# Down projection of a Strassen-like FFN: result tiles taken at the first write, and the combinations of w_out on VectorE, one step ahead of their split

## The chip, the cores and the metric

The kernel runs on one core of one Trainium2 chip. The metric is device time in microseconds of one execution, the median of several runs. One profiled execution gives the trace. The engines are TensorE (PE in the profile), VectorE (DVE), ScalarE (ACT), GpSimd (POOL) and SyncE (SP), which issues the DMAs. Each engine works through its own instructions strictly in order, and engines wait for one another on semaphores.

## The reference

A trunk of two layers on 1024 positions of width 1024, all in fp32. Layer 0 mixes tokens by a gated MLP, layer 1 by RWKV-7; each then has cross-attention to a small memory and a SwiGLU FFN with D_FF = 2816, each part between two RMS norms and added to x. The part that matters here is the FFN, which runs twice:

```python
def swiglu_ffn(x, w_in, w_out):
    gate, up = jnp.split(x @ w_in, 2, axis=-1)
    return (jax.nn.silu(gate) * up) @ w_out
```

The change touches the last product, h @ w_out, with h of 1024 x 2816 and w_out of 2816 x 1024: the down projection.

## The kernel before

**Splits.** Matrix products work on fp32 numbers taken apart into a high and a low part of a shorter format. `split` makes them: ScalarE copies the source into the high part (`wh`, L118), VectorE subtracts it from the source and so gets the low part (`wl`, L119). Three matmuls (high by high, high by low, low by high) then stand for one.

**Seven products.** The down projection divides h and w_out into 2 x 2 blocks and forms seven products of sums of blocks, in Strassen's manner, where plain blocks would need eight. The combinations of h are made in `ffn`, by GpSimd, and written to seven scratch arrays in DRAM (L485 to L501). `ffn_out` does the rest. It runs the products in the order 1, 2, 5, 6, 3, 7, 4. Each has six steps along the inner dimension: the first of one 128-row piece (tiles of 128x512), the five others of two (128x1024). So there are 42 steps, numbered q, and each has 12 or 24 matmuls into four PSUM banks of 128x512, one for each j of 0 to 3. Banks `A` serve products 1, 6, 7 and 4, banks `B` the products 2, 5 and 3.

**One round of the loop, step q:**

- `load(q + 3)` has SyncE fetch the step's piece of h into a `wr` tile (three buffers, L596). In products 1, 2, 5 and 6 it also fetches a piece of w_out into an `a32` tile (L600), kept for the products after. Each of these four products brings in one of the four blocks of w_out.
- `unit(q + 1)` first makes the combination of w_out that the step needs, in place, as the difference of two kept pieces: L609 in product 5, L611 in 6, L613 in 7, L615 in 4. The engine `E` is GpSimd. It then splits the piece of h (`wl<-wr`) and that of w_out (`wl<-a`); there are buffers for two steps' parts.
- `mm` (L634) does the matmuls of step q, and after a product's last step `evac` takes the four banks' results into the result tiles `y`: a copy by ScalarE in products 1, 5 and 6, an addition by VectorE in products 2 (L657), 3 (L664) and 7 (L667).
- A result half that is final goes to `finish`: ScalarE sums its squares (L646), VectorE multiplies it by a gain (L647), and when a tile is whole, a closing task for the norm and the addition to x is queued and worked off in `tick`.

**Buffers.** All 128x1024 fp32 tiles of this part (`a32`: h's tiles, pieces of w_out, results) come from one pool, `A`, of 32 buffers. Whoever takes one waits until its last user is done. The eight result tiles are taken at the start of `ffn_out` (L588).

**Order.** The program's text gives the order in which work is handed out, but a scheduler in the compiler's front end orders each engine's instructions by a simulated timeline. A change in one place can so reorder instructions elsewhere.

In the second FFN (`by_tile`) the last product runs tile by tile at the end, with splits that stay resident.

## Time and profile before

| | us |
|---|---|
| median of 3 runs (3232.7 to 3247.02) | 3232.87 |
| the profiled execution's own time | 3235.78 |
| its span, first to last instruction | 3234.0 |
| first down projection, on TensorE | about 1081 to 1320 |
| second down projection, on TensorE | about 2992 to 3226 |
| mean granted clock of TensorE | 0.969 |

The page of the profile gives for each engine its busy time, share of the span and instructions. Groups of instructions read "line, engine, operation, out<-in, shapes, count | busy us, mean ns of one | idle time before them and what ended it". Timeline rows read "start, duration, engine, line, operation, count [idle time before <- what ended it]". Rows of waits read "who waits <- for whom: us in total, times, longest". Rows of windows give the busy time of engines in a stretch, TensorE's granted clock, the DMA share and the rate.

### The profile page before, as it was taken

Reading aid. Unit: us, or ns where it says so; the run is one execution under the profiler, and the core shown is the slowest. Engines: PE = TensorE matmul, PEld = TensorE weight load, DVE = VectorE, ACT = ScalarE, POOL = GpSimd, SP = SyncE. Lnnn points to the kernel's source line nnn. Section 1 sums busy time; section 2 is a strip of 40 time slices with the busy share of each in tenths; the row PEclk is TensorE's granted clock in tenths of the full one; section 3 lists DMA queues with packets and bytes.
Section 4 is the critical chain, followed back from the end, with each engine's and each line's share of the span. In section 5 each row is a group of like instructions: output and inputs, shape, how many; then the busy total and the mean of one; then the engine's idle time right before and its main releaser. Section 6 shows DMA issues by size and latency. Waiting matters only on the chain. (4 is left out here: it accounts for less than half of the span.)

```text
span 3234.0 us, 44200 instructions
## 1 busy us (share of the span) xinstructions
PE 3082.2 (95%) x16570; PEld 2514.8 (78%) x16570; DVE 1864.5 (58%) x2626; ACT 1484.1 (46%) x2751; POOL 1033.2 (32%) x810
## 2 busy tenths in 40 slices
PE   8999999899999989999989899999999899999998
PEld 6888888778888767878767788887788688887776
DVE  5563544665555486655765677565545755554766
ACT  5442544533333335666753355465545533332433
POOL 0100011365555270111421443333011655554441
PEclk9999999999999999999998889799999999999999
DMA  5622644423333634644866634535554233333633
GB/s 190 206 74 70 199 125 154 143 73 103 101 98 100 249 123 130 203 140 144 263 197 191 186 95 111 142 96 186 176 164 155 66 102 98 98 104 129 220 103 138
DMA packets 432502, 456.56 MB, mean 141 GB/s; under 512 B 77664, under 2 KB 307200, under 8 KB 432288
## 3 DMA queue, kind: packets, MB, share of 16 engines
q1 hardware_dynamic: 425376, 428.57, 41.9%
q0 software_dynamic: 6912, 25.17, 2.4%
q8 instruction: 131, 2.15, 0.3%
q14 instruction: 83, 0.68, 0.1%
HBM read 331.43 MB, written 122.22 MB: 140 GB/s over the span
## 5 line engine op out<-in xcount | busy, mean ns | idle before, releaser
L119 DVE TENSOR_TENSOR wl<-wr,wh 128x1024 fp32r<-128x1024 f32 (+1 forms) x417 | 514.7, 1244 | 472.9 <-ACT wh L118 472.0
L438 PE MATMUL ps<-a,wh 128*128 128x512 f32 x2464 | 771.0, 398 | 8.4 <-DVE a L119 6.2
L118 ACT CAST wh<-wr 128x1024 fp32r<-128x1024 f32 (+1 forms) x417 | 371.2, 902 | 638.1 <-PE ps L634 194.9
L438 PEld LDWEIGHTS ps<-a,wh 128*128 128x128 f32 x2464 | 464.8, 189 | 125.9 <-DVE a L119 8.0
L438 PE MATMUL ps<-a,wl 128*128 128x512 f32 x1232 | 479.7, 398 | 0.0
L148 PE MATMUL ps<-a,wh 128*128 128x512 f32 (+1 forms) x848 | 328.6, 392 | 13.1 <-ACT a L118 9.6
L148 PE MATMUL ps<-wh,a 128*128 128x512 f32 x800 | 315.8, 402 | 12.4 <-ACT t L1159 3.3
L150 PE MATMUL ps<-a,wl 128*128 128x512 f32 (+1 forms) x848 | 325.0, 385 | 1.6 <-DVE wl L119 1.5
L149 PE MATMUL ps<-a,wh 128*128 128x512 f32 (+1 forms) x848 | 324.9, 384 | 1.1 <-DVE a L119 1.1
L149 PE MATMUL ps<-wl,a 128*128 128x512 f32 x800 | 318.6, 398 | 0.6 <-DVE wl L119 0.6
L150 PE MATMUL ps<-wh,a 128*128 128x512 f32 x800 | 316.4, 399 | 0.0
L208 POOL TENSOR_TENSOR sm<-sm,mhalf 128x4 f32<-128x4 f32 (+3 forms) x60 | 71.7, 1196 | 676.4 <-DVE sm L228 606.3
L438 PEld LDWEIGHTS ps<-a,wl 128*128 128x128 f32 x1232 | 232.8, 189 | 57.4 <-DVE wl L119 0.9
L634 PE MATMUL ps<-wl,wh 128*128 128x512 f32 x588 | 236.0, 401 | 21.2 <-DVE wl L119 21.1
L119 DVE TENSOR_TENSOR wl<-s,wh 128x512 fp32r<-128x512 f32 x176 | 200.2, 1151 | 64.0 <-ACT wh L118 60.4
L634 PE MATMUL ps<-wh,wl 128*128 128x512 f32 x588 | 233.1, 396 | 0.0
L634 PE MATMUL ps<-wh 128*128 128x512 f32 x588 | 197.1, 398 | 18.1 <-ACT wh L118 13.0
L148 PEld LDWEIGHTS ps<-a,wh 128*128 128x128 f32 x848 | 162.2, 192 | 45.8 <-ACT a L118 10.5
L118 ACT CAST wh<-s 128x512 fp32r<-128x512 f32 x176 | 106.3, 619 | 198.9 <-PE ps L438 70.9
L150 PEld LDWEIGHTS ps<-a,wl 128*128 128x128 f32 x848 | 162.4, 192 | 35.9 <-DVE wl L119 2.8
L148 PEld LDWEIGHTS ps<-wh,a 128*128 128x128 f32 x800 | 151.6, 190 | 49.7 <-ACT t L1159 3.8
L149 PEld LDWEIGHTS ps<-a,wh 128*128 128x128 f32 x848 | 163.1, 192 | 31.8 <-DVE a L119 1.5
(281 smaller groups left out, 5562.0 us busy)
## 6 DMA issues: line engine op xcount, KB each, us to landing
scr<-a SPq DMA_DIRECT2D x218, 256.0 KB
wr<-in_ffn_w_in SPq DMA_DIRECT2D x90, 512.0 KB
wr<-scr SPq DMA_DIRECT2D x70, 512.0 KB
scr<-t SPq DMA_DIRECT2D x60, 512.0 KB
wr<-in_rw_w_rkv SPq DMA_DIRECT2D x48, 512.0 KB
a<-in_ffn_w_out SPq DMA_DIRECT2D x40, 512.0 KB
t<-scr SPq DMA_DIRECT2D x36, 512.0 KB
ld<-scr SPq DMA_DIRECT2D x72, 256.0 KB
```

The source lines that it names most:

```text
L118: self.nc.scalar.copy(hi, src)
L119: (engine or self.nc.vector).tensor_sub(lo, src, hi)
L148: nc.tensor.matmul(out, lhsT=ah, rhs=bh, start=start, stop=False)
L149: nc.tensor.matmul(out, lhsT=ah, rhs=bl, start=False, stop=False)
L150: nc.tensor.matmul(out, lhsT=al, rhs=bh, start=False, stop=stop)
L208: self.nc.gpsimd.tensor_tensor(out=r, in0=v, in1=self.mhalf[:, 0:n], op=ALU.pow)
L438: self.nc.tensor.matmul(out, lhsT=a, rhs=b, start=start and k == 0 and (i == 0), stop=k == 3 and i == 2, skip_group_check=True)
L634: nc.tensor.matmul(ps, lhsT=a, rhs=b, start=i in (1, 2, 5) and n == 0 and k == 0 and z == 0, stop=n == NS - 1 and k == steps[n][1] - 1 and ...
```

## The change

Two edits in `ffn_out`, made together.

First, the result tiles: `y` starts empty, and `evac` takes a tile from pool `A` when it is first written, in product 1 (upper row of blocks) and in product 5 (lower row).

Second, the combinations: they leave `unit` for a function of their own, `combine`, which uses VectorE. The loop calls it for step q + 2, ahead of `unit(q + 1)`. So a combination is handed out one round before the split that reads it.

```diff
-        y = [self.a32() for _ in range(NT)]
+        y = {}
...
-        def unit(q, resident=False):
+        def combine(q):
+
             i, n = seq[q]
-            K = steps[n][1]
-            N = K * 512
-            w = lambda b, a: W[b, a, n][:, :N]
-            E = nc.gpsimd
+            w = lambda b, a: W[b, a, n][:, :steps[n][1] * 512]
+            E = nc.vector
             if i == 5:
                 E.tensor_sub(w(0, 0), w(0, 1), w(0, 0))
             elif i == 6:
...
             elif i == 4:
                 E.tensor_sub(w(1, 0), w(1, 0), w(0, 0))
+
+        def unit(q, resident=False):
+            i, n = seq[q]
+            K = steps[n][1]
+            N = K * 512
+            w = lambda b, a: W[b, a, n][:, :N]
             src = {1: (0, 0), 5: (0, 0), 6: (0, 0), 2: (1, 0), 4: (1, 0), 3: (1, 1), 7: (0, 1)}[i]
...
         def evac(i, j, A, B):
             o = lambda r, c: y[2 * j + r][:, c * 512:c * 512 + 512]
+            if i in (1, 5):
+                y[2 * j + i // 5] = self.a32()
             if i == 1:
...
                 load(q + AHEAD)
+            if q + 2 < len(seq):
+                combine(q + 2)
             if q + 1 < len(seq):
                 unit(q + 1, by_tile and seq[q + 1][0] == 4 and seq[q + 1][1] < NS - 2)
```

In the changed kernel the combinations stand at L608, L610, L612 and L614, `mm` at L639, the squares at L651, the gain at L652, the additions at L664 (product 2), L671 (3) and L674 (7). Each pass has 24 combinations; 24 instructions so leave GpSimd and 24 join VectorE.

How the program's order on an engine moves is shown below; a row has the line, the operation, the tiles with their numbers (`out<-in`), and the shape. Tile numbers differ between the two programs.

The first place is VectorE in the first FFN, at the end of product 2 and the start of product 5. Before: the splits of product 5's first step, then the additions and gains of product 2's results with the splits of the second step between them.

```order
L119 TENSOR_TENSOR wl_8582<-wr_8504,wh_8581 128x512
L119 TENSOR_TENSOR wl_8586<-a_8174,wh_8585 128x512
L657 TENSOR_TENSOR a_8162<-ps_8416,a_8162 128x512
L657 TENSOR_TENSOR a_8164<-ps_8420,a_8164 128x512
L647 TENSOR_TENSOR a_8162<-a_8162,gb_8170 128x512
L657 TENSOR_TENSOR a_8166<-ps_8424,a_8166 128x512
L647 TENSOR_TENSOR a_8164<-a_8164,gb_8170 128x512
L657 TENSOR_TENSOR a_8168<-ps_8428,a_8168 128x512
L119 TENSOR_TENSOR wl_8633<-wr_8540,wh_8632 128x1024
L647 TENSOR_TENSOR a_8166<-a_8166,gb_8170 128x512
L119 TENSOR_TENSOR wl_8637<-a_8178,wh_8636 128x1024
```

The same place of the change (L664 are the additions, L652 the gains).

```order
L119 TENSOR_TENSOR wl_8579<-wr_8500,wh_8578 128x512
L119 TENSOR_TENSOR wl_8583<-a_8166,wh_8582 128x512
L610 TENSOR_TENSOR a_8166<-a_8729,a_8166 128x512
L664 TENSOR_TENSOR a_8374<-ps_8412,a_8374 128x512
L614 TENSOR_TENSOR a_8286<-a_8286,a_8166 128x512
L664 TENSOR_TENSOR a_8382<-ps_8416,a_8382 128x512
L652 TENSOR_TENSOR a_8374<-a_8374,gb_8162 128x512
L664 TENSOR_TENSOR a_8390<-ps_8420,a_8390 128x512
L652 TENSOR_TENSOR a_8382<-a_8382,gb_8162 128x512
L664 TENSOR_TENSOR a_8398<-ps_8424,a_8398 128x512
L119 TENSOR_TENSOR wl_8630<-wr_8536,wh_8629 128x1024
L119 TENSOR_TENSOR wl_8634<-a_8170,wh_8633 128x1024
```

The first combinations of products 6 (L610) and 4 (L614) have come in among the additions; the one for product 4 is made here already. Those of product 5 (L608) and the first three of product 7 (L612) stand some rows further up, between product 2's splits.

The second place is VectorE at steps 1 to 3 of product 6. Before: splits alone, that of h's piece and that of w_out's in turn.

```order
L119 TENSOR_TENSOR wl_8851<-wr_8767,wh_8850 128x1024
L119 TENSOR_TENSOR wl_8855<-a_8178,wh_8854 128x1024
L119 TENSOR_TENSOR wl_8876<-wr_8804,wh_8875 128x1024
L119 TENSOR_TENSOR wl_8880<-a_8182,wh_8879 128x1024
L119 TENSOR_TENSOR wl_8913<-wr_8845,wh_8912 128x1024
L119 TENSOR_TENSOR wl_8917<-a_8194,wh_8916 128x1024
```

The same place of the change, from the second of these splits to the fifth.

```order
L119 TENSOR_TENSOR wl_8856<-a_8170,wh_8855 128x1024
L610 TENSOR_TENSOR a_8186<-a_8848,a_8186 128x1024
L612 TENSOR_TENSOR a_8626<-a_8848,a_8626 128x1024
L119 TENSOR_TENSOR wl_8877<-wr_8801,wh_8876 128x1024
L610 TENSOR_TENSOR a_8214<-a_8873,a_8214 128x1024
L612 TENSOR_TENSOR a_8655<-a_8873,a_8655 128x1024
L119 TENSOR_TENSOR wl_8881<-a_8174,wh_8880 128x1024
L614 TENSOR_TENSOR a_8402<-a_8402,a_8186 128x1024
L610 TENSOR_TENSOR a_8250<-a_8910,a_8250 128x1024
L612 TENSOR_TENSOR a_8692<-a_8910,a_8692 128x1024
L614 TENSOR_TENSOR a_8430<-a_8430,a_8214 128x1024
L119 TENSOR_TENSOR wl_8914<-wr_8846,wh_8913 128x1024
```

Two combinations stand ahead of the splits of step 2, two between them, and four ahead of those of step 3, which read `a_8848`, `a_8873` and `a_8910`, the last three pieces of w_out to be loaded.

The third place is SyncE at the start of the first down projection. Before: the store of h's last parts (`scr`) and the loads of w_out.

```order
L369 DMA t4_9331<-scr2_93 128x1024
L490 DMA scr12_4981<-a_8115 128x512
L491 DMA scr14_4983<-a_8115 128x512
L600 DMA a_8174<-in_ffn_w_out 128x512
L495 DMA scr15_4984<-a_8153 128x512
L600 DMA a_8178<-in_ffn_w_out 128x2x512
```

The same place of the change.

```order
L369 DMA t4_9332<-scr2_93 128x1024
L490 DMA scr12_4981<-a_8115 128x512
L491 DMA scr14_4983<-a_8115 128x512
L600 DMA a_8166<-in_ffn_w_out 128x512
L495 DMA scr15_4984<-a_8153 128x512
L600 DMA a_8170<-in_ffn_w_out 128x2x512
```

Only the numbers of the tiles have moved.

## The prediction

> **What bounds the kernel now.** First the page: the share of each engine, and the chain that ended last.

> ```profile
> span 3234.0 us, 44200 instructions
> PE 3082.2 (95%) x16570; PEld 2514.8 (78%) x16570; DVE 1864.5 (58%) x2626; ACT 1484.1 (46%) x2751; POOL 1033.2 (32%) x810
> PE 35%; DVE 3%; DMA 2%; ACT 1%; issue 1%; POOL 0%; SPq 0%; DVEq 0%; POOLq 0%; ACTq 0%
> ```

> TensorE is busy for 95% of the span, so an edit that removes no matmul can win only from the remaining 152 us of idle time and from a low clock. Next, what TensorE waits for in the down projection (L634), over the whole span; the columns are total us, times and the longest wait.

> ```profile
> PE ps L634 <- DVE wl L119: 21.1, 18, 2.7
> PE ps L634 <- ACT wh L118: 13.0, 3, 6.4
> PE ps L634 <- DVE a L657: 5.1, 6, 1.4
> ```

> That is 39 us in two passes, and no row has GpSimd as releaser: where the combinations are made, TensorE waits for a split (`wl`) or for an addition into a result tile (`a`, L657), both on VectorE. The timeline of TensorE shows where these waits lie in the first pass (seven of the ten after 1130 us; in brackets the idle time).

> ```profile
> 1133.65 0.50 PE L634 MATMUL ps<-wl,wh 128*128 128x512 f32 x1 [0.42 <-DVE wl L119]
> 1145.53 0.47 PE L634 MATMUL ps<-wh 128*128 128x512 f32 x1 [1.44 <-DVE a L657]
> ...
> 1152.09 0.49 PE L634 MATMUL ps<-wl,wh 128*128 128x512 f32 x1 [0.98 <-DVE wl L119]
> 1159.37 0.50 PE L634 MATMUL ps<-wl,wh 128*128 128x512 f32 x1 [1.54 <-DVE wl L119]
> 1186.08 0.50 PE L634 MATMUL ps<-wl,wh 128*128 128x512 f32 x1 [1.86 <-DVE wl L119]
> 1199.41 0.50 PE L634 MATMUL ps<-wl,wh 128*128 128x512 f32 x1 [0.52 <-DVE wl L119]
> ...
> 1212.75 0.50 PE L634 MATMUL ps<-wl,wh 128*128 128x512 f32 x1 [0.90 <-DVE wl L119]
> ```

> They form two zones, and the waits by window give their sums: 1130 to 1165 us (end of product 2, product 5), then 1183 to 1215 us (product 6), then the same zones of the second pass (3042 to 3080, where the L657 row repeats, and 3094 to 3127).

> ```profile
> PE ps L634 <- DVE wl L119: 2.9, 3, 1.5
> PE ps L634 <- DVE a L657: 2.5, 3, 1.4
> PE ps L634 <- DVE wl L119: 4.2, 4, 1.9
> PE ps L634 <- DVE wl L119: 3.3, 3, 1.5
> PE ps L634 <- DVE wl L119: 4.4, 4, 2.0
> ```

> Why VectorE is late there: groups of its splits in 1110 to 1215 us, where the combinations run, and in 1215 to 1244 us, where none does; then one place in the timeline.

> ```profile
> L119 DVE TENSOR_TENSOR wl<-a,wh 128x1024 fp32r<-128x1024 f32 x15 | 38.8, 2589 | 0.4 <-ACT wh L118 0.4
> L119 DVE TENSOR_TENSOR wl<-a,wh 128x1024 fp32r<-128x1024 f32 x5 | 6.1, 1220 | 0.2 <-ACT wh L118 0.2
> 1181.49 3.46 POOL L611 TENSOR_TENSOR a<-a 128x1024 f32<-128x1024 f32 x1 [15.43 <-DMA a<-in_ffn_w_out]
> 1182.89 3.14 DVE L119 TENSOR_TENSOR wl<-a,wh 128x1024 fp32r<-128x1024 f32 x1 [0.20 <-ACT wh L118]
> 1185.95 3.38 DVE L119 TENSOR_TENSOR wl<-wr,wh 128x1024 fp32r<-128x1024 f32 x1
> ```

> The same split takes 1.22 us alone and 3.4 us beside a GpSimd combination. While both engines run, VectorE falls behind; that is the bound of these zones, about 20 us of idle time in all.

> **The change part by part.** *Taking result tiles late* frees eight of 32 buffers while product 1 begins. The 6.4-us waits at the start of each pass are for `wh`, and ACT in its turn had waited for the first w_out load:

> ```profile
> 1080.62 0.62 ACT L118 CAST wh<-a 128x512 fp32r<-128x512 f32 x1 [7.59 <-DMA a<-in_ffn_w_out]
> ```

> In SyncE's order that load still stands behind the same write of h's parts, and the matmuls it waits for are the same. So I take 0. The bounds are 0 and a gain of the whole 13.0 us; a loss is excluded, since no load is placed later.

> *Moving the combinations* takes 48 instructions off GpSimd and puts as many of the same shapes on VectorE. GpSimd's groups of 12 run from 2.84 to 3.10 us each:

> ```profile
> L613 POOL TENSOR_TENSOR a<-a 128x1024 f32<-128x1024 f32 (+1 forms) x12 | 37.1, 3104 | 0.0
> L611 POOL TENSOR_TENSOR a<-a 128x1024 f32<-128x1024 f32 (+1 forms) x12 | 34.1, 2843 | 43.9 <-DVE wl L119 28.4 <-DMA a<-in_ffn_w_out 15.4
> ```

> No combination runs on VectorE before. The nearest rows are its own fp32 subtractions of the same shapes, undisturbed:

> ```profile
> 1175.59 0.69 DVE L119 TENSOR_TENSOR wl<-wr,wh 128x512 fp32r<-128x512 f32 x1 [2.65 <-ACT wh L118]
> 1221.20 1.23 DVE L119 TENSOR_TENSOR wl<-wr,wh 128x1024 fp32r<-128x1024 f32 x1
> 1222.34 1.22 DVE L119 TENSOR_TENSOR wl<-a,wh 128x1024 fp32r<-128x1024 f32 x1
> ```

> Back to back they start 1.14 us apart; the small shape's pair 0.6 us. The ends for one combination are 1.14 us and, if it ran as on GpSimd, 3.4 us; I take 1.14, the row of the same engine and operation. Per pass this adds 20 x 1.14 + 4 x 0.6 = 25 us to VectorE, and takes away 15 x (2.59 - 1.22) = 20 us on the `a` splits and about 14 us on the `wr` splits, which are slowed alike. So VectorE gets no busier; what matters is where the combinations stand.

> *Zone of product 5.* Idle is 5.4 us in the first pass and 5.8 in the second. Each wait also restarts TensorE slowly: its first matmul takes 0.50 us instead of 0.39 and the next start slips, 0.28 us a wait, six waits, 1.7 us. Together 7.1 and 7.5 us. After: the last result of product 2 ends about 1143.7 on TensorE; VectorE adds it (0.6), then makes the two splits of step 1 (2 x 1.14), ending 1146.7. TensorE would ask for them at 1146.0, so one wait of about 0.8 us stays, 1.1 with its restart. The five others go: their splits now precede the demand by 1 to 2 us. Saved **6.0 and 6.4 us**.

> *Zone of product 6.* Idle 4.2 and 4.4, four restarts 1.1, and the clock fell after the longest wait. Windows of 2 us, with TensorE's busy time, granted clock, DMA share and GB/s, first at a wait of 1.54 us, then after that of 1.86:

> ```profile
> 1158.00:1160.00 2.00, 0.63 (x3) 1.00 0.53 206
> 1186.00:1188.00 2.00, 1.92 (x6) 0.72 0.47 167
> 1188.00:1190.00 2.00, 2.00 (x6) 0.50 0.33 127
> 1190.00:1192.00 2.00, 2.00 (x10) 0.92 0.67 242
> 1186.88 0.61 PE L634 MATMUL ps<-wl,wh 128*128 128x512 f32 x1
> ...
> 1190.28 0.41 PE L634 MATMUL ps<-wh,wl 128*128 128x512 f32 x1
> ```

> In the last two rows eight starts lie 0.425 us apart instead of 0.227: 1.6 us lost. The zone costs 6.9 and 7.1 us. The waits of 1.44 and 1.54 us left it at 1.00, so I take 1.54 as safe.

> [...]

> After: nine combinations stand among the first splits of product 6. From 1182.89: the split of step 1 ends 1184.05, when TensorE asks (1184.2): no wait. Two combinations, a split, two combinations, the split of step 2: six at 1.14 end 1190.9; TensorE asks at 1189.5, a wait of 1.4. Four combinations and two splits end 1197.8; it asks at 1196.6, 1.2. Later splits have nothing ahead of them. 2.8 us with restarts stay, no wait as long as 1.54, so the clock holds. Saved **4.1 and 4.3 us**.

> *Waits added.* A combination of product 5 or of 7 waits on VectorE for its w_out load, and the splits queue behind it, then TensorE. Two places:

> ```profile
> 1117.96 17.89 POOL L609 TENSOR_TENSOR a<-a 128x512 f32<-128x512 f32 x6 [36.78 <-DMA a<-in_ffn_w_out]
> 1176.71 1.49 SPq L600 DMA_DIRECT2D a<-in_ffn_w_out  x3
> ```

> Before, the operands were there at 1117.96 and then kept pace with six combinations; VectorE reaches its first at 1119 and the sixth about 1129. The three last loads were in use from 1181.49, and VectorE reaches them at 1184.05. So 0, with 2.5 us of slack; beyond it each us late is a us lost.

> *The rest.* The wait of up to 2.7 us at product 3, and what else stays of the `wl` row, stands beside the closing work, not touched: 0. The scheduler also reorders parts of the RWKV layer; there the largest wait (1400 to 2500 us) is

> ```profile
> PE ps L148 <- ACT a L118: 10.2, 4, 5.4
> ```

> and the waits add to some 50 us. I take 0, with 5 us either way, a tenth of them.

> Sum: 6.0 + 6.4 + 4.1 + 4.3 = 20.8 us. The profiled execution took 3235.8 us (span 3234.0 and 1.8 around it): 3215.0. It lies 2.9 above the median of 3232.87, so the forecast is **3212**, -0.6%. A difference below 0.5% (16 us) can hardly be told from none.

> **The rivals.** *Half is given back.* The two waits left in product 6 last longer than 1.5 us and the clock falls once or twice in each pass (1.6 us each, 3 to 6 in all), or the saving of the first pass shrinks at the DMA-bound places of the next layer, and only 10 to 14 us come: 3219 to 3222, within 0.5%. For it: the margins above are 0.1 to 1.4 us. Against it: the second pass has nothing behind it.

> *Slower: a combination is as dear on VectorE as on GpSimd.* Then the burst of product 6 decides. TensorE's waits at steps 2 and 3 are each four combinations and two splits less one step of TensorE (24 matmuls, 5.45 us): 4c + 2.28 - 5.45 for a combination of c us. At 1.14 that is the 1.4 above, at 3.4 it is 10.4 twice, 21 us a pass with 0.6 for restarts and 1.6 or more for the clock, against 7 before, and the 20 us more of VectorE use up the gain at product 5 too. Two passes: 3233 + 2 x 17 = 3267. The gain of the two passes, 20.8, is gone when 16 x (c - 1.14) reaches it: at 2.4 us. Against it: the undisturbed rows at 1.22.

> *VectorE stops at a load.* If the last three loads land later than 1184.05 on that clock, the combinations wait, with them the splits of steps 1 to 3, and TensorE loses each us one to one. The gain of a pass is gone when they land at 1194; at 1200 in both passes the time is 3212 + 2 x 16 = 3244. For it: on SyncE they stand behind loads of h that wait for splits. Against it: in the profile they are issued 4.8 us before first use, and their order stays.

> *The late result tiles do pay:* the first loads gain their buffers earlier and the 6.4-us waits go: 3212 - 13 = 3199. Against it: SyncE's order.

> **How the numbers follow.** Forecast as summed, within 5 us: 0.56. Half given back: 0.24. Dear combinations: 0.04. Stopped at a load: 0.08. Result tiles pay: 0.08. The range 3201 to 3229 takes in the forecast, half given back and the small cases of either; it leaves out the dear combinations, most of the stop, and the lower end of the last. Faster by over 0.5% (below 3216.7) holds the forecast but for its upper edge, and the last rival: 0.61; within 0.5%: half given back, that edge and the milder stops, 0.31; slower: 0.08.

> **What would show it.** Right: no GpSimd work from these lines; splits at 1.22 us in both zones; combinations at 1.2 us; waits of L634 on `wl` at about 10 us instead of 21, on the additions near 0, on `wh` still 13; granted clock 1.00 in product 6. Wrong: combinations over 2 us, a DMA of w_out as a releaser on VectorE, waits for `wh` gone, or new waits of TensorE in the RWKV layer.

## The result and the profile after

| | before | after |
|---|---|---|
| median of 9 runs, us | 3240.79 | 3220.90 |
| all runs, us | 3232.7 to 3250.6 | 3208.5 to 3226.1 |
| profiled execution, us (span) | 3235.78 (3234.0) | 3209.03 (3207.3) |
| first pass, first to last matmul of `mm`, us | 233.05 | 221.76 |
| second pass, us | 234.08 | 220.83 |
| from the first pass to the second, us | 1678.2 | 1675.2 |

The ratio of the runs is **0.993, 95% interval 0.9912 to 0.9948**: faster by 0.7%, where 3212 of 3232.87, 0.9935, was forecast. Both medians lie 8 to 9 us above the values that the prediction started from and arrived at, 3232.87 and 3212, since its three runs of the kernel before lay low. A few runs of these kernels took over 5900 us; they are left out of every median and ratio here.

The page of the kernel after, its span and engines:

```profile
span 3207.3 us, 44170 instructions
PE 3071.3 (96%) x16570; PEld 2511.4 (78%) x16570; DVE 1829.9 (57%) x2674; ACT 1484.9 (46%) x2751; POOL 893.0 (28%) x762
```

GpSimd has lost its 48 instructions and 140 us; VectorE has 48 more and is busy 35 us less. The waits of TensorE in the down projection (L639 now) over the whole span:

```profile
PE ps L639 <- ACT wh L118: 13.2, 3, 6.4
...
PE ps L639 <- DVE wl L119: 11.9, 9, 2.7
```

The waits for `wh` stay at 13; those for `wl` fall from 21.1 to 11.9, and the row of the additions into result tiles after product 2 (5.1 before) is gone. The timeline of TensorE has these waits of 0.3 us and more in the first pass, after the 6.43 at its start:

```profile
1184.59 0.50 PE L639 MATMUL ps<-wl,wh 128*128 128x512 f32 x1 [1.09 <-DVE wl L119]
1191.40 0.50 PE L639 MATMUL ps<-wl,wh 128*128 128x512 f32 x1 [1.05 <-DVE wl L119]
1243.59 0.50 PE L639 MATMUL ps<-wl,wh 128*128 128x512 f32 x1 [2.63 <-DVE wl L119]
1258.01 0.50 PE L639 MATMUL ps<-wl,wh 128*128 128x512 f32 x1 [1.49 <-DVE wl L119]
```

Nothing is left in the zone of product 5, two waits in that of product 6, and the long one of product 3 is as before. VectorE's groups show why: splits in 1110 to 1205 us, then two of the four groups of combinations over the whole span.

```profile
L119 DVE TENSOR_TENSOR wl<-wr,wh 128x1024 fp32r<-128x1024 f32 x15 | 18.3, 1220 | 17.3 <-ACT wh L118 17.2
L119 DVE TENSOR_TENSOR wl<-a,wh 128x1024 fp32r<-128x1024 f32 x15 | 18.3, 1218 | 0.4 <-ACT wh L118 0.4
L612 DVE TENSOR_TENSOR a<-a 128x1024 f32<-128x1024 f32 (+1 forms) x12 | 13.4, 1128 | 0.0
L608 DVE TENSOR_TENSOR a<-a 128x1024 f32<-128x1024 f32 (+1 forms) x12 | 13.1, 1129 | 0.0
```

In the kernel before, 15 splits of each kind took 2.59 (`wl<-a`) and 2.18 us (`wl<-wr`) in 1110 to 1215 us. VectorE did not stand idle ahead of these combinations (0.0), and by 0.1 us in all ahead of the other two groups: none waited for its load.

### The profile page after: what moved, and what is told of

Same layout as the page of the kernel before. It is cut to its first block, busy times and chain, and to the rows that moved or that the text cites. A ratio compares the mean times of both kernels' runs of the same rounds, so it can differ in the third digit from the quotient of the medians.

```text
span 3207.3 us, 44170 instructions
## 1 busy us (share of the span) xinstructions
PE 3071.3 (96%) x16570; PEld 2511.4 (78%) x16570; DVE 1829.9 (57%) x2674; ACT 1484.9 (46%) x2751; POOL 893.0 (28%) x762
## 5 line engine op out<-in xcount | busy, mean ns | idle before, releaser
L119 DVE TENSOR_TENSOR wl<-wr,wh 128x1024 fp32r<-128x1024 f32 (+1 forms) x417 | 477.6, 1155 | 480.1 <-ACT wh L118 477.3
L118 ACT CAST wh<-wr 128x1024 fp32r<-128x1024 f32 (+1 forms) x417 | 371.1, 901 | 621.3 <-PE ps L639 172.3
L148 PE MATMUL ps<-a,wh 128*128 128x512 f32 (+1 forms) x848 | 328.3, 392 | 11.2 <-ACT a L118 7.9
L148 PE MATMUL ps<-wh,a 128*128 128x512 f32 x800 | 314.5, 401 | 11.7 <-ACT t L1168 3.0
L438 PEld LDWEIGHTS ps<-a,wl 128*128 128x128 f32 x1232 | 233.0, 189 | 57.2 <-DVE wl L119 0.9
L639 PE MATMUL ps<-wl,wh 128*128 128x512 f32 x588 | 231.9, 394 | 11.9 <-DVE wl L119 11.9
L119 DVE TENSOR_TENSOR wl<-s,wh 128x512 fp32r<-128x512 f32 x176 | 199.8, 1149 | 67.5 <-ACT wh L118 64.2
L639 PE MATMUL ps<-wh,wl 128*128 128x512 f32 x588 | 229.9, 391 | 0.0
L639 PE MATMUL ps<-wh 128*128 128x512 f32 x588 | 194.8, 394 | 13.2 <-ACT wh L118 13.2
L118 ACT CAST wh<-s 128x512 fp32r<-128x512 f32 x176 | 106.4, 620 | 199.7 <-PE ps L438 66.7
L148 PEld LDWEIGHTS ps<-a,wh 128*128 128x128 f32 x848 | 162.1, 192 | 44.3 <-ACT a L118 8.8
L148 PEld LDWEIGHTS ps<-wh,a 128*128 128x128 f32 x800 | 151.3, 189 | 48.5 <-ACT t L1168 3.5
```

Source lines behind the costliest of these rows:

```text
L118: self.nc.scalar.copy(hi, src)
L119: (engine or self.nc.vector).tensor_sub(lo, src, hi)
L148: nc.tensor.matmul(out, lhsT=ah, rhs=bh, start=start, stop=False)
L438: self.nc.tensor.matmul(out, lhsT=a, rhs=b, start=start and k == 0 and (i == 0), stop=k == 3 and i == 2, skip_group_check=True)
L639: nc.tensor.matmul(ps, lhsT=a, rhs=b, start=i in (1, 2, 5) and n == 0 and k == 0 and z == 0, stop=n == NS - 1 and k == steps[n][1] - 1 and ...
```

## The experiments

**The result tiles alone.** The kernel before with `y = {}` and the tile taken in `evac`:

```diff
-        y = [self.a32() for _ in range(NT)]
+        y = {}
...
+            if i in (1, 5):
+                y[2 * j + i // 5] = self.a32()
```

> The kernel before with the late result tiles alone. Theory of the prediction: worth nothing, within 2 us of the kernel before; the two waits of L634-like matmuls for wh at the start of the passes stay at 6.4 us each, and the ten waits on VectorE after 1130 us stay at 19.9 us in all. Rival (the tiles give the first loads their buffers): the waits for wh go, 13 us faster.

Measured: 1.0005 of before (0.9991 to 1.0019). TensorE's waits in its profile, over the whole span:

```profile
PE ps L634 <- DVE wl L119: 21.7, 17, 4.0
PE ps L634 <- ACT wh L118: 12.8, 2, 6.4
...
PE ps L634 <- DVE a L659: 5.1, 6, 1.5
```

They are those of before. This edit is worth nothing by itself, and the rival falls. One wait differs, 4.0 us where before had 1.86, and its place shows what the order of the two engines' starts did. The timeline of GpSimd, VectorE and TensorE at step 1 of product 6:

```profile
1182.82 2.41 POOL L611 TENSOR_TENSOR a<-a 128x1024 f32<-128x1024 f32 x1 [15.28 <-DMA a<-in_ffn_w_out]
1182.95 3.37 DVE L119 TENSOR_TENSOR wl<-wr,wh 128x1024 fp32r<-128x1024 f32 x1 [4.57 <-ACT wh L118]
1189.65 0.80 PE L634 MATMUL ps<-wl,wh 128*128 128x512 f32 x1 [3.95 <-DVE wl L119]
```

Here GpSimd began 0.13 us ahead of the step's first split, and that split took 3.37 us. In the kernel before it had begun 0.03 us behind it (1181.49), and the split ran undisturbed:

```profile
1181.46 1.22 DVE L119 TENSOR_TENSOR wl<-wr,wh 128x1024 fp32r<-128x1024 f32 x1 [4.58 <-ACT wh L118]
```

So TensorE waited 2.1 us longer here. In both cases the one that began second took longer, by about what the other still had to do: here the split, 3.37 us instead of 1.22, with 2.28 us of the GpSimd instruction to come; in the kernel before GpSimd, 3.46 us instead of 2.41, with 1.19 us of the split to come. What the two engines share is not shown by these runs.

**VectorE, but no step ahead.** The kernel before with one word changed:

```diff
-            E = nc.gpsimd
+            E = nc.vector
```

> The kernel before with the combinations on VectorE, but still handed out in the round of their split, and the result tiles taken up front. Theory (the engine is what counts, since splits beside a GpSimd combination take 3.4 us instead of 1.2): as the change, 20 to 25 us faster than before in the profile, about 0.993; waits on the first additions gone, two waits of about 1 us at product 6 in each pass. Rival (the step ahead is what counts): a combination directly ahead of its split delays it by 1.14 us or more at each of 24 steps, so that half of the gain or more is missing, 3222 or slower.

Measured: 0.9954 (0.9933 to 0.9975). The passes take 222.4 and 222.6 us, 22 less than before together. Of the waits in 1130 to 1215 us one row is left:

```profile
PE ps L634 <- DVE wl L119: 2.1, 2, 1.1
```

This is the row of the change. The scheduler hoists the combinations on VectorE by itself, to nearly the same places: the first ones of the burst in product 6 start at 1179.93, in the change at 1177.64, both right behind a split of w_out's piece. The median, 3223.8, is some 3 us above that of the change, and the intervals overlap: the step ahead adds nothing that these runs can tell.

**One step ahead, but on GpSimd.** The change with its engine set back, and the tiles up front:

```diff
-            E = nc.vector
+            E = nc.gpsimd
...
-        y = {}
+        y = [self.a32() for _ in range(NT)]
```

> The kernel before with the combinations one step ahead, still on GpSimd. Theory: the splits still run beside GpSimd combinations at 3.4 us, so nothing is won: within 5 us of before, waits of the down projection on VectorE 17 to 23 us as before. Rival (TensorE waits because a combination comes late): most of the gain of the change, 15 us or more.

Measured: 1.0015 (0.9994 to 1.0035); passes of 234.0 and 234.2 us; waits for splits of 20.3 us over the span. First the splits in 1110 to 1215 us, then the waits in 1130 to 1218:

```profile
L119 DVE TENSOR_TENSOR wl<-a,wh 128x1024 fp32r<-128x1024 f32 x15 | 38.8, 2588 | 0.4 <-ACT wh L118 0.4
PE ps L639 <- DVE wl L119: 7.2, 7, 1.9
PE ps L639 <- DVE a L662: 2.6, 3, 1.5
```

Splits and waits are those of before. The rival falls: that the combination came late was not the trouble.

**No combinations at all.** The four branches are taken out of the kernel before:

```diff
-            if i == 5:
-                E.tensor_sub(w(0, 0), w(0, 1), w(0, 0))
...
-                E.tensor_sub(w(1, 0), w(1, 0), w(0, 0))
```

> The kernel before with all 48 combinations of w_out left out (the products use the uncombined blocks). Theory: every wait of the two zones goes, with restarts and clock 14 us in each pass, 28 us: about 3208 in the profile, some 4 us less than the change; splits at 1.22 us throughout. Rival (VectorE is slow there for another reason, such as the w_out loads arriving at 390 GB/s): splits of 1110 to 1140 us still above 2 us and waits of 5 us or more left in the zones.

This leaves 48 subtractions out of the computation. Measured: 0.9915 (0.9893 to 0.9936); passes of 219.9 and 220.9 us, and one wait of 0.2 us between 1130 and 1215 us. In 1110 to 1205 us its splits took 1.22 us, with the loads of w_out as before, so it is not the loads that slow them. The combinations thus cost the kernel before 26.3 us in its two passes, and the change wins back 24.5. Part of both is the clock after the wait at product 3, which fell in both passes of before, in one here and in none of the change (last section): at 1.7 us each, 24.6 and 21.1 us remain.

**The change with duplicates on GpSimd.** Each combination is made a second time, into a tile that nobody reads:

```diff
+        dup = self.s7.tile([P, D], F32, name='s7', tag='s7')
...
+            pair = {5: ((0, 1), (0, 0)), 6: ((1, 1), (0, 0)), 7: ((1, 1), (0, 1)), 4: ((1, 0), (0, 0))}.get(i)
+            if pair:
+                nc.gpsimd.tensor_sub(dup[:, :steps[n][1] * 512], w(*pair[0]), w(*pair[1]))
```

> The change, and GpSimd makes each of the 24 differences of a pass a second time into a spare tile that nobody reads; nothing but buffers of operands waits for it. Theory (VectorE and GpSimd slow each other down whenever both run such subtractions): splits and combinations of VectorE beside the duplicates at 2.5 to 3.4 us again, in 79 us of a pass some 45 instructions of VectorE fewer, less its idle time: TensorE's waits grow by 20 to 45 us a pass, 3250 to 3300. Rival (before, TensorE waited because GpSimd's result came late): nobody waits for the duplicates, within 5 us of the change.

Measured: 1.0147 (1.0118 to 1.0175), median 3287.7. Groups of GpSimd and VectorE, then TensorE's waits, over the span:

```profile
L618 POOL TENSOR_TENSOR s<-a 128x1024 f32<-128x1024 f32 (+1 forms) x48 | 154.0, 3207 | 167.5 <-DVE a L609 87.3 <-DVE a L611 70.7 <-issue 7.0
L615 DVE TENSOR_TENSOR a<-a 128x1024 f32<-128x1024 f32 x10 | 20.8, 2082 | 0.0
L609 DVE TENSOR_TENSOR a<-a 128x1024 f32<-128x1024 f32 x10 | 20.5, 2081 | 0.0
PE ps L643 <- DVE wl L119: 50.5, 17, 6.7
```

Work whose result nobody reads makes the kernel 66 us slower than the change (3221 to 3222 in its two measurements), and no wait of VectorE in the passes names a duplicate as what ended it. VectorE's combinations of products 5 and 4 go from 1.22 to 2.08 us (those of 6 and 7 stay at 1.21), and the waits on its splits from 11.9 to 50.5. Up to half of the 66 us is the clock that fell at the longer waits: summed from the granted clock, 36 us are lost to it in the two passes, 4 in the change.

**Loads six steps ahead.** The w_out part of `load` becomes a function of its own:

```diff
+        def load_w(q):
...
+            if q + 6 < len(seq):
+                load_w(q + 6)
```

> The change with the pieces of w_out loaded six steps ahead instead of three, so that the last three stand on SyncE ahead of the loads of h and the nine combinations of product 6 need not be made in one burst. Theory (the two waits left at product 6 come from the burst): they go, 2.7 us a pass, and nothing else moves: 5 us faster than the change. Rival (VectorE stops at a load): the loads of 1110 to 1130 us already run at 390 GB/s, 1.5 MB more take 4 us, and combinations that stand ahead of product 2's splits wait for them: new waits of TensorE of 1 to 4 us between 1130 and 1145 us, no gain or slower.

Measured: 0.9966 (0.9942 to 0.9989), a median of 3238.1 and so **slower** than the change by 16 us instead of faster by 5, though the intervals overlap. Yet its passes take 219.3 and 219.8 us, and in 3030 to 3150 us one wait is left (none in 1120 to 1235):

```profile
PE ps L643 <- DVE wl L119: 0.3, 1, 0.3
```

So the two waits of product 6 did come from the burst, and no load stops VectorE; the time went elsewhere, into the 1698 us between the passes.

**The first loads early.** In the FFN's last block, ahead of its last stores:

```diff
+            if m == NF - 1:
+                self.W0 = []
...
+                for c, K in ((0, 1), (1, 2), (3, 2))[:3]:
+                    t = self.a32()
+                    nc.sync.dma_start(t[:, :K * 512].rearrange('p (k c) -> p k c', k=K), wv[0][:, c:c + K, 0:512])
+                    self.W0.append(t)
```

> The change with the first three loads of w_out handed out during the last block of the FFN's first half, ahead of the stores of h's last parts on SyncE. Theory (the 6.4-us wait at the start of a pass is for a load that stands too far back in SyncE's order, not for buffers): the wait falls below 2 us, and the low clock after it goes for the most part: 5 to 8 us a pass, 10 to 16 us faster than the change. Rival (the first piece of h or the next pieces of w_out are as late): waits at the first two steps that add to 4 us or more, gain below 5 us in all.

Measured: 0.993 (0.9905 to 0.9956), runs from 3201 to 3238; the median, 3217.2, is 5 us under the change's, where 10 to 16 were expected. The row of waits for `wh` is gone altogether, and the first pass ends at 1295.0 us instead of 1303.9. In the profiled execution, one of 3235.2 us, all of it is lost again between the passes. First the longest wait in 1990 to 2100 us, in the RWKV layer, with its row in the timeline; then TensorE in 5 us ahead of it and in 100 us around it (busy, granted clock, DMA share, GB/s); then the same stretch of the change:

```profile
PE ck L1426 <- DMA x<-scr: 6.2, 1, 6.2
2019.52 0.98 PE L1426 MATMUL ck<-x 32*32 32x32 f32 x50 [6.25 <-DMA x<-scr]
2000.00:2005.00 5.00, 4.53 (x29) 0.58 0.39 120
1995.00:2095.00 100.00, 91.89 (x739) 0.57 0.49 128
2000.00:2100.00 100.00, 95.43 (x1119) 0.95 0.53 140
```

The clock stayed at half for 85 of the 100 us. The wait of 6.2 us did not start this: a mean of 0.58 over 2000 to 2005 puts the fall at about 2000.8, and the wait began at 2013.3.

**The change again.**

> The change once more, as it stands, for the comparison with the two above and for a second profile. Theory: the same waits to 0.2 us (1.1 twice at product 6, 2.6 at product 3), about 0.993 of before. What may differ is the clock: if a stretch of low clock begins only where more than some 1.7 us of one cell of a fixed 3.41-us raster are idle, the 2.6-us wait lowers it in some passes and not in others, and every stretch ends on the same raster. Rival (the length of the wait alone decides): as in the first profile, no low clock after 2.6 us.

Measured: 0.9934 (0.9912 to 0.9956), passes of 221.8 and 221.85 us, the same waits in both zones. In neither pass did the clock fall after the 2.6 us at product 3, so this run by itself does not decide between the two readings of the clock; all profiles together do (last section). From 1304.6 to 2990.3, between the passes, it took 1685.7 us, 10.5 more than in the first profile of the very same kernel. I summed the time lost to the clock there from 40 windows, each its length times one less its granted clock. It is 74 us in the first profile of the change and 85 in the second, 79 in that of before, 93 with loads six steps ahead, 118 with the first loads early. What remains of the stretch is 1591 to 1605 us in all five. So the clock makes most of the difference between runs.

**The change in one pass alone.** The change also moves the scheduler's order in the RWKV layer, as the early loads do (the order of VectorE's instructions there differs from that of before); made in the second FFN alone it doesn't. So two kernels have the change in one pass each:

```diff
+        new = self.nf == 2
+        y = {} if new else [self.a32() for _ in range(NT)]
...
-            E = nc.vector
+            E = nc.vector if new else nc.gpsimd
...
+            if new and q + 2 < len(seq):
+                combine(q + 2)
+            elif not new and q + 1 < len(seq):
+                combine(q + 1)
```

> The change in the second FFN alone; the first FFN and every row of the RWKV layer on TensorE stand in the order of the kernel before. Theory: the second pass takes 221 to 223 us instead of 234, the rest is that of before: 12 us faster, 0.996. Rival (the order of the layer between the passes makes a good part of the gain): 8 us or less.

> The change in the first FFN alone; the RWKV layer stands in the order of the change. Theory: the first pass takes 222 to 223 us instead of 233, and the gain is carried through the next layer whole: 11 us faster, 0.9965. Rival (half given back: what the first pass wins is lost in the next layer): 5 us or less. Second rival (the next layer gains by its new order): 16 us or more.

Measured: the second pass alone 0.9974 (0.9954 to 0.9993), the first alone 0.9971 (0.9942 to 1.0). The changed pass takes 222.1 and 222.3 us, the other 233.0 and 234.4. Each is worth 8 to 9 us by its ratio, less than the 11 to 12 of the pass, and together they make 0.9945, within the change's own interval. The ratios alone can't exclude that some is lost: the first interval holds gains from 2 to 15 us, the second from none to 19. The profiles say more. By the same sum as above, the stretch between the passes without its time lost to the clock is 1596 us with the change in the first pass alone and 1599 in the kernel before, so that apart from the clock nothing of the first pass's gain is lost there.

**The early loads in the second pass alone,** so that the RWKV layer keeps the order of the change: both edits of the loads, under `self.nf == 2`.

> The change, and in the second FFN alone the first three loads of w_out early and the others six steps ahead, so that the layer before it keeps the order of the change. Theory (the medians of the two kernels with early loads were spoilt by low clock in the RWKV layer, not by the loads): second pass without the waits of 6.4 and twice 1.1 us, 10 us faster than the change, 0.990 of before. Rival (the early loads themselves cost as much elsewhere): as the change, 0.993 or more.

Measured: 0.9891 (0.9863 to 0.9919), median 3206.1. The wait of 6.4 us ahead of the second pass is gone, in 2960 to 3120 us one wait is left, and the RWKV stretch (1996 to 2096) is as in the change:

```profile
PE ps L654 <- DVE wl L119: 0.3, 1, 0.3
1996.00:2096.00 100.00, 95.72 (x1135) 0.97 0.53 141
```

> The kernel of e11 once more. Theory (ten us of its lead over the change are real): 0.988 to 0.991 of before. Rival (e11 drew fast runs): 0.992 or more. What its profile has of low clock in the RWKV layer may differ from e11's, as it did between two profiles of the change (74 and 85 us lost).

Measured: 0.9901 (0.9871 to 0.993), median 3212.4. Both lie below 0.993, and this version has the lowest medians of all kernels with the whole computation: 1.0% under before. The intervals (0.9863 to 0.9919, 0.9871 to 0.993) still touch those of the change. The second pass itself takes 221.5 and 221.4 us, about as in the change: the two waits that are gone are offset by the clock, which fell after product 3 in both profiles and in neither of the change's. The gain lies ahead of the pass: without the time lost to the clock, the stretch between the passes takes 1591 us in both profiles, where the change's two have 1601.

## Why the prediction was right, and where it was off

**The bound and its cause** held. VectorE was late because its splits ran beside GpSimd: 2.59 us for a `wl<-a` split in 1110 to 1215 us, 1.22 after the change. Three runs single this out: the engine alone gives the gain, the earlier step on GpSimd gives none, and duplicates on GpSimd take it away. A fourth, without any combination, has the splits at 1.22 us.

**The price of a combination** held: in the burst of product 6 they start 1.14 us apart, as taken from the splits.

```profile
1177.64 1.22 DVE L610 TENSOR_TENSOR a<-a 128x1024 f32<-128x1024 f32 x1
1178.78 1.22 DVE L612 TENSOR_TENSOR a<-a 128x1024 f32<-128x1024 f32 x1
```

That it could be as dear as on GpSimd was refuted.

**The zone of product 5** was sized at 6.0 and 6.4 us; the whole 7.1 and 7.5 came. The step that failed was "one wait of about 0.8 us stays". VectorE ended the split where forecast, at 1147.54 in a pass that starts 0.83 us later. TensorE, in the rows under it, asked for it only then:

```profile
1146.32 1.22 DVE L119 TENSOR_TENSOR wl<-a,wh 128x1024 fp32r<-128x1024 f32 x1
1146.57 1.07 PE L639 MATMUL ps<-wh 128*128 128x512 f32 x4
1147.59 0.50 PE L639 MATMUL ps<-wl,wh 128*128 128x512 f32 x1
```

It ran four matmuls of high parts first, as it does in the kernel before, so its demand comes about 0.7 us later than I had put it. That no wait at all is left is luck: the split ended 0.05 us ahead of the matmul that reads it.

**The zone of product 6** was forecast with waits of 1.4 and 1.2; they are 1.09 and 1.05. With two restarts of 0.28 us, the prediction's estimate, 2.7 us stay, and 4.2 and 4.5 were saved where 4.1 and 4.3 were forecast. The clock held there (1.00 over 1184 to 1192 us).

**Product 3, "not touched: 0"**, failed. Its wait of 2.6 us stayed, but in the kernel before the clock fell after it, and in the kernel after it didn't. Windows of before, then of after:

```profile
1256.00:1258.00 2.00, 2.00 (x6) 0.50 0.42 68
1242.00:1244.00 2.00, 0.41 (x2) 1.00 1.03 406
1244.00:1246.00 2.00, 2.00 (x11) 1.00 0.51 205
```

That is 1.7 us in each pass, 3.4 us of the difference between the two profiles. It was not forecast, and it is luck: in both passes of the change a boundary of the clock's raster cut the wait in two (below). A wait of 1.49 us is new in the first pass, 1.8 with its restart. There two closing instructions stand between the splits on VectorE:

```profile
1253.22 1.22 DVE L119 TENSOR_TENSOR wl<-wr,wh 128x1024 fp32r<-128x1024 f32 x1
1254.35 2.47 DVE L378 SCALAR_TENSOR_TENSOR t<-a,sm,t 128x1024 f32<-128x1024 f32 x2
1256.74 1.22 DVE L119 TENSOR_TENSOR wl<-a,wh 128x1024 fp32r<-128x1024 f32 x1
```

Sum of the passes: 14.6 at product 5, 8.7 at product 6, 3.4 of the clock, less 1.8: 24.9, where the passes show 24.5 and 20.8 was forecast. Without the clock's 3.4 the passes show 21.1. That this lies so near to 20.8 is in part luck too: 2.5 us too little at products 5 and 6 and the new wait of 1.8 nearly cancel. By the medians the gain is 20 us. The time lost to the clock between the passes differs by 11 us in two profiles of the change (74 and 85), so that these numbers do not contradict one another. The median itself, 3220.9, lies where the prediction had put *half is given back* (3219 to 3222), but only because the kernel before is 8 us slower than its first three runs.

**The result tiles at 0** held: the waits of 6.4 us stayed. They were for the place of the first loads in SyncE's order, as the early loads show, where they are gone.

**The rivals.** "Half is given back" is not borne out: the clock held at product 6, and the stretch between the passes takes no longer, apart from the clock, with the change in the first pass alone. "Stopped at a load" did not come, not even with the loads handed out six steps ahead.

## What to carry to other kernels

Look not only at what an engine waits for but at how long its own instructions take beside another engine's: here a split of 1.22 us took up to 3.4 while GpSimd ran the same kind of work, and with that work moved to VectorE, the *busier* of the two, VectorE was busy 1829.9 us instead of 1864.5. An edit that saves a few microseconds in one place can reorder the rest of a scheduled program, so compare stage by stage, and confine an edit to the last stage to see what it is worth alone. When runs of one kernel spread by 18 us, sum the granted clock by stage before arguing from two profiles.

## What the runs showed of the hardware

**In these profiles the clock fell by a raster, not by the length of a wait.** The prediction took waits up to 1.54 us as safe from what two of them left. Waits of that length did leave the clock alone, but length by itself did not decide: 1.86 us lowered the clock, and 2.63 us in the change did not. Windows of 1 us in the kernel before, at the ends of the first pass's stretches of low clock and, in the second row, at a start:

```profile
1084.00:1085.00 1.00, 1.00 (x5) 0.75 0.94 356
1186.00:1187.00 1.00, 0.92 (x4) 0.95 0.17 64
1190.00:1191.00 1.00, 1.00 (x6) 0.85 0.33 102
1258.00:1259.00 1.00, 1.00 (x5) 0.71 0.99 383
```

**Long low clock beside small matmuls is not explained.** In the RWKV layer, where TensorE runs many small matmuls, the kernel with the first loads early spent 85 of 100 us at half clock, though TensorE's records show it busy 92% of the time. The share of the passes did not hold there: the clock fell at 2000.8 after a cell with at most 1.2 us idle, and it stayed low behind cells without any idle time on record (2022 to 2040 us: busy for all 18, clock 0.50). What kept it low these runs do not show. Whether the order of that layer in the kernels with early loads brought this about more often, or their runs drew it by chance, was not settled: the five profiles have 74 to 118 us lost there, two profiles of one kernel already differ by 11.
